# Strassen over all tokens for the output projection, and the second norm inside the MLP

## The chip, the cores and the metric

The kernel runs on one core of a Trainium2 chip. The metric is the device time of one execution in microseconds (us), given as the median of several runs. A profile of one execution is used to see where the time goes. The engines are TensorE (PE; its weight loads are PEld), VectorE (DVE), ScalarE (ACT), GpSimd (POOL) and SyncE (SP), which here issues nearly all transfers.

## The reference, cut to what matters

One decoder layer for 1024 tokens of width 1024: a norm and one large projection, two attention branches, their gated merge, an output projection with a residual, and an MLP of width 4096 with a squared relu. The change lies in the last lines.

```python
merged = g_a * (o_a @ w_up_dil) + g_b * (o_b @ w_up_sb)     # (1024 tokens, 1024)
x  = x + merged @ w_out                                      # output projection
h2 = rmsnorm(x, norm_mlp_g)                                  # x * rsqrt(mean(x*x) + eps) * g
x  = x + jnp.square(jax.nn.relu(h2 @ w_mlp_in)) @ w_mlp_out  # MLP
return rmsnorm(x, norm_final_g)
```

## The kernel before, in words

**Number format.** Everything is held transposed: features on the 128 partitions, tokens along the free axis, in tiles of 128 x 512. A product in float32 accuracy is made of three matmuls. Each operand is split into a high half (a ScalarE copy into the rounded type fp32r) and a low half (a VectorE subtraction, operand minus high half); the three are high x high, high x low and low x high (`mm3`, `product`). So each operand of each product costs one ScalarE and one VectorE operation.

**Strassen.** Large products use the Strassen-Winograd form on 2 x 2 blocks: seven block products in place of eight, with four sums or differences of the left (weight) blocks, `s1` to `s4` (`lefts`), four of the right (activation) blocks, `t1` to `t4`, and additions of the results. A *pair* is two output tiles. The products are taken in the order 0, 1, 5, 6, 4, 3, 2; products 0 and 1 need only plain blocks, and the others need sums or differences.

**Stages after the attention.** (1) The up products of the stick-breaking branch: for each of 8 tiles and each half of the tokens (`c`), 12 matmuls, then a VectorE multiplication with the gate and an addition give `mg[c][j]`. (2) The output projection. For the tokens 0 to 511 it is Strassen with the token halves 0 to 255 and 256 to 511 as the two block columns (`out_pair`); POOL makes its differences `t1` to `t4` (tiles `tw`, `WC[0]` is 'p'), and VectorE the sums of weights. For the tokens 512 to 1023 it is plain, in two quarters of 256 tokens. Each result is added to a tile `x1` of the residual, which also goes to memory (`xdr`). (3) The second norm: for each of the three parts of the tokens, `squares` sums the squares over the features (ScalarE squares, VectorE adds over groups of `GW` tiles, a matmul with ones sums over partitions, tile `ss`), `rstd` takes the root and spreads it over the partitions by a matmul with the identity (tile `rb`), and VectorE multiplies `x1` by the gain and by `rb`. (4) From these normalized tiles come the seven right operands `hm` of the hidden layer (`operands`), for the last 512 tokens in two halves. (5) The hidden layer has 16 pairs of 84 matmuls each (7 products of 4 k and 3 matmuls). The first products (0 and 1) of `NE` = 4 pairs are begun early, before the operands 2 to 6 are ready (`hidden_first`, `hidden_11`). `finish` is relu and square, both on ScalarE; for the block `b12` it is a ScalarE relu and a VectorE multiplication. The results go to memory (`udr`). (6) The down projection, Strassen too, and the final norm.

**The order of the work.** Nothing is issued where the program text stands. Each call is recorded in a plan (`Plan.record`), and `Plan.issue` places the instructions on the engines by a list schedule: TensorE's recorded order gives each matmul a position in time, every other instruction a due time worked back from what needs it, and an engine takes the ready instruction that is due first. Three limits hold it: a window by engine (how far ahead of the oldest unstarted instruction it may reach; `WMLP` holds after the attention), a slack added to the due times, and the tiles: 102 slots of 128 x 512 (`NSLOT`) and 8 banks of PSUM. All instructions are issued through one helper, so every row of the profile has the line L388, and the rows are told apart by the names of tiles: `bank` is an accumulator, `ws` a block of weights with its sums and halves, `gl` the gated products, `msh`/`msl` the halves of `mg`, `hh`/`hl` the halves of the hidden layer's operands, `pk` a hidden block, `x` a tile of the residual, `sq` squares.

Of the kernel before, what the change touches and what calls it, by code (L numbers as in the profile page):

```python
# [9 lines left out]
F32 = mybir.dt.float32  # L10
# [29 lines left out]
MC = 0  # L40
OPE = "pd"
HPE = (0, 0)
DPE = "d"
WC = 'pd'
# [9 lines left out]
GW = 8  # L54
GT = 8
LW = False
# [5 lines left out]
WMLP = {'pe': 45000.0, 'act': 15000.0, 'dve': 40000.0, 'pool': 30000.0, 'sync': 40000.0}  # L62
# [4 lines left out]
NE = 4  # L67
FIRST = 2
STEPS = (1, 3, 4, 5, 6)
EARLY = (5, 6, 7, 7, 7)  # L70
# [321 lines left out]
def hybrid_block(ctx, tc, xT, w_t, w_vn, w_up, w_o, w_mi, w_mo, gains, bgate, out):  # L392
# [861 lines left out]

    plan.window = WMLP
    mg = [[None] * 8 for _ in range(2)]
# [8 lines left out]
    for c, j in [(c, j) for c in range(2) for j in range(8)] if MC else [(c, j) for j in range(8) for c in range(2)]:  # L1265
        if c == 0:
            wu[j] = weight(w_up[j][:, 2:6], 4, "wu", e=WLE[2])
        ps = bank()
        proj(ps, wu[j], oo[c])
        gt = gated(ps, 1, j, c)  # L1270
        dve.tensor_add(gt, gt, ga[c][j])
        mg[c][j] = gt if c == 0 else split(gt, "ms")
# [5 lines left out]
    wo = [None] * 8  # L1278
    x1 = [[None] * 8 for _ in range(2)]
    h2 = [u2("h2n", F32) for _ in range(8)]  # L1280
    hm = [None] * 7

    def finish(t):
        act.activation(t, t, AF.Relu)
        act.activation(t, t, AF.Square)
# [5 lines left out]
    def hidden_11(m, b0, b1):  # L1291
        product(b0, m[0], hm[0], True)
        b11 = keep(b0)
        product(b1, m[1], hm[1], True)
        dve.tensor_add(b11, b11, b1)
        finish(b11)
        return b11

    def pairs():
        return [u2("tc", F32).rearrange("p (k t) -> p k t", k=2) for _ in range(2)]  # L1300

    def one(ts):
        return [t[:, i] for t in ts for i in range(2)]

    def operands(b12, b22, sl, e):

        t1, t2, t3, t4 = (pairs() for _ in range(4))

        def sub(d, x, y):
            for i in range(len(d)):  # L1310
                e.tensor_sub(d[i], x[i], y[i])

        def part(m, t):
            for (hi, lo), x in zip(hm[m], one(t)):
                act.activation(hi[:, sl], x, AF.Copy)
                dve.tensor_sub(lo[:, sl], x, f(hi[:, sl]))

        sub(one(t1), one(b12), [t[:, sl] for t in h2[0:4]])
        sub(t2, b22, t1)
        part(5, t2)  # L1320
        yield
        sub(t3, b22, b12)
        part(6, t3)
        yield
        part(4, t1)
        yield
        sub(one(t4), [t[:, sl] for t in h2[4:8]], one(t2))
        part(3, t4)
        yield
        part(2, b22)  # L1330


    def wide():
        return u2("tw", F32).rearrange("p (k t) -> p k t", k=2)

    def parts(ts):

        return [(x[0][:, i], x[1][:, i]) for x in [halve3(t) for t in ts] for i in range(2)]

    def halve3(t):  # L1340
        hi, lo = (u2("tw").rearrange("p (k t) -> p k t", k=2) for _ in range(2))
        act.activation(hi, t, AF.Copy)
        dve.tensor_sub(lo, t, f(hi))
        return hi, lo

    tw = [[wide() for _ in range(2)] for _ in range(4)]
    top = [(t[:, 0:256], t[:, 256:512]) for t in mg[0]]
    low = [(u2("msh"), u2("msl")) for _ in range(4)]
    for k in range(4):
        (b11, b12), (b21, b22) = top[k], top[k + 4]  # L1350
        t1, t2, t3, t4 = (t[k // 2][:, k % 2] for t in tw)
        for d, x, y in ((t1, b12, b11), (t2, b22, t1), (t3, b22, b12), (t4, b21, t2)):
            eng(WC[0]).tensor_sub(d, x, y)
    first = []
    for k in range(4):
        hi, lo = u2("msh"), u2("msl")
        act.activation(hi[:, 0:256], top[k][0], AF.Copy)
        dve.tensor_sub(lo[:, 0:256], top[k][0], f(hi[:, 0:256]))
        first.append((hi[:, 0:256], lo[:, 0:256]))
    for k in range(4):  # L1360
        act.activation(low[k][0], mg[0][k + 4], AF.Copy)
        dve.tensor_sub(low[k][1], mg[0][k + 4], f(low[k][0]))
    wr = [first] + [[(hi[:, 256 * i:256 * i + 256], lo[:, 256 * i:256 * i + 256]) for hi, lo in low] for i in range(2)]
    p1, p2, p3, p4 = (parts(tw[m]) for m in range(4))
    wr = [wr[0], wr[1], wr[2], p4, p1, p2, p3]

    def out_pair(j):

        for i in range(2):
            x1[0][j + i] = u2("x1", F32)  # L1370
            sync.dma_start(x1[0][j + i], xT[j + i, :, 0:512])
        blocks = load_blocks([w_o[j + i][:, 4 * m:4 * m + 4] for i in range(2) for m in range(2)])
        am = lefts(*blocks, eng=eng(WC[1]))
        for i, pair in ((0, (am[0], am[1])), (1, (halve_w(blocks[2]), am[3]))):
            wo[j + i] = [(hi[:, k], lo[:, k]) for hi, lo in pair for k in range(4)]
        b0, b1, b2 = (bank()[:, 0:256] for _ in range(3))
        for b, m, n, i, h in ((b0, 0, 1, 0, 0), (b1, 1, 1, 0, 0), (b0, 5, 0, 1, 0), (b2, 6, 1, 1, 1), (b0, 4, 0, 1, 1),
                              (b2, 3, 0, 1, 0), (b0, 2, 0, 0, 1)):
            product(b, am[m], wr[m], n > 0)
            xt = x1[0][j + i][:, 256 * h:256 * h + 256]  # L1380
            dve.tensor_add(xt, xt, b)

    for c, o, n in ((0, 0, 512), (1, 0, 256), (1, 256, 256)):
        ssq, add = squares(n // 128, 8, GW, LW and o > 0)
        cs = slice(o, o + n)
        if o:
            early = []
            for m in range(2, 7):
                hm[m] = [(u2("hh"), u2("hl")) for _ in range(4)]
            steps = operands(*later, slice(0, 256), eng(OPE[0]))  # L1390
        for j in range(8):
            if c == 0 and j % 2 == 0:
                out_pair(j)
            if o == 0 and c:
                x1[c][j] = u2("x1", F32)
                sync.dma_start(x1[c][j], xT[j, :, 512 * c:512 * c + 512])
            xt = x1[c][j][:, cs]
            if c:
                ps = bank()[:, 0:n]
                proj(ps, wo[j], [(x[0][:, cs], x[1][:, cs]) for x in mg[c]])  # L1400
                dve.tensor_add(xt, xt, ps)
            if o + n == 512:
                sync.dma_start(xdr[c, j], x1[c][j])
            add(xt)
            if o:
                if j in STEPS:
                    next(steps, None)
                while len(early) < NE and j >= EARLY[len(early)]:
                    early.append(hidden_first(len(early)))
        rs, _ = rstd(ssq, n // 128)  # L1410
        if o:
            early = [(m, b0, hidden_11(m, b0, b1)) for m, b0, b1 in early]

# [206 lines left out]
```

## Time and profile before

| | us |
|---|---|
| median of 3 runs | 1456.57 (1455.22 to 1458.94) |
| the profiled execution | 1458.5 |
| its span, first to last instruction | 1456.7 |
| TensorE matmul busy in the span | 1422.6 (98%) |
| VectorE busy | 1144.7 (79%) |
| ScalarE busy | 784.9 (54%) |
| POOL busy | 202.5 (14%) |

Matmuls are pipelined: a matmul's recorded time overlaps the next one's, so TensorE's rate is read from the distance between starts. A row of the profile names an operation as *out<-in*, gives the shape, the number of such operations, their busy time, the mean length of one in ns, and the idle time of the engine before them with what ended it.

### The profile page before, as it was taken

To read this page: it belongs to the slowest core of one execution; us is meant where nothing else is said; L and a number is where in the kernel's file an instruction comes from. 1 tells how busy PE (TensorE), PEld (TensorE's weight loads), DVE (VectorE), ACT (ScalarE), POOL (GpSimd) and SP (SyncE) were. 2 spreads that over 40 slices of the span, in tenths; PEclk is the share of its full clock that TensorE was granted. 3 is DMA by queue.
4 is the path that set the end of the run, shared out by engine and by line. 5 is a ranking of instruction groups with operands and counts; after the bars stand their busy time and mean duration, and the time that the engine had idled before them with its cause. 6 is when DMAs were issued, how large, how long until landed. Compare 5 with 4: busy or idle time off the path is not lost.

```text
span 1456.7 us, 21968 instructions
## 1 busy us (share of the span) xinstructions
PE 1422.6 (98%) x7432; PEld 1209.7 (83%) x7432; DVE 1144.7 (79%) x1968; ACT 784.9 (54%) x1650; POOL 202.5 (14%) x196
## 2 busy tenths in 40 slices
PE   9999999999999998999999999999999999999997
PEld 9987888888788876888889978888888788888887
DVE  7876887776887868789898898666666969798976
ACT  7656776664655544585453565544555625252632
POOL 2452322322311232010210300000000000000000
PEclk9999999999999999999999999999999999999999
DMA  6247646665245624568032435444446945362703
GB/s 225 65 155 249 209 156 217 218 230 192 64 143 181 200 91 132 178 205 299 32 105 84 162 116 181 148 154 155 148 152 233 345 128 189 104 215 65 253 1 116
DMA packets 133808, 236.60 MB, mean 162 GB/s; under 512 B 16608, under 2 KB 24128, under 8 KB 133696
## 3 DMA queue, kind: packets, MB, share of 16 engines
q1 hardware_dynamic: 131648, 228.91, 46.6%
q0 software_dynamic: 2048, 6.29, 1.4%
q8 instruction: 58, 0.95, 0.3%
q14 instruction: 54, 0.44, 0.1%
HBM read 160.03 MB, written 75.12 MB: 161 GB/s over the span
## 4 chain that ended last, share of the span: by engine, by line
PE 87%; DMA 5%; DVE 4%; ACT 1%; issue 1%; SPq 0%; POOL 0%; DVEq 0%; ACTq 0%; POOLq 0%
PE bank L388 72%; PE vps L388 5%; PE po L388 3%; PE sc L388 3%; PE tr L388 3%; DMA qs<-pdr 1%; DMA pdr<-pl 1%; DVE be L388 1%; DMA pdr<-ph 1%; DVE ws L388 1%; DMA gdr<-gt 0%; SPq L388 0%; PE rb L388 0%; DMA udil<-ut 0%; DVE tw L388 0%
## 5 line engine op out<-in xcount | busy, mean ns | idle before, releaser
L388 PE MATMUL bank<-hh,ws 128*128 128x512 f32 x2016 | 647.2, 394 | 5.1 <-DVE pk L388 4.2
L388 PEld LDWEIGHTS bank<-hh,ws 128*128 128x128 f32 x2016 | 376.4, 188 | 82.1 <-DVE pk L388 5.3
L388 PE MATMUL bank<-hl,ws 128*128 128x512 f32 x1008 | 396.8, 394 | 0.0
L388 DVE TENSOR_TENSOR ws<-ws 128x512 fp32r<-128x512 f32 (+1 forms) x540 | 363.5, 707 | 39.0 <-ACT ws L388 15.5
L388 ACT ACTIVATE ws<-ws 128x512 fp32r<-128x512 f32 x396 | 232.8, 624 | 133.6 <-DVE ws L388 87.7
L388 PE MATMUL bank<-hi,ws 128*128 128x512 f32 (+1 forms) x960 | 281.6, 377 | 2.0 <-DVE x L388 2.0
L388 PEld LDWEIGHTS bank<-hl,ws 128*128 128x128 f32 x1008 | 190.1, 189 | 36.6
L388 PEld LDWEIGHTS bank<-hi,ws 128*128 128x128 f32 x960 | 177.1, 189 | 35.4 <-DVE x L388 2.4
L388 PE MATMUL bank<-lo,ws 128*128 128x512 f32 (+1 forms) x480 | 180.7, 376 | 0.0
L388 POOL TENSOR_TENSOR ws<-ws 128x512 f32<-128x512 f32 x80 | 118.5, 1489 | 329.5 <-DVE ws L388 63.3
L388 DVE TENSOR_TENSOR pk<-pk,bank 128x512 f32<-128x512 f32 x108 | 74.0, 686 | 87.4 <-PE bank L388 63.8
L388 DVE TENSOR_TENSOR x<-x,bank 128x512 f32<-128x512 f32 (+1 forms) x164 | 95.7, 587 | 54.9 <-PE bank L388 54.5
L388 ACT ACTIVATE pk<-bank 128x512 f32<-128x512 f32 x110 | 65.4, 595 | 91.8 <-PE bank L388 79.6
L388 ACT ACTIVATE pk<-pk 128x512 f32<-128x512 f32 x96 | 60.3, 628 | 84.0 <-DVE pk L388 83.5
L388 PEld LDWEIGHTS bank<-lo,ws 128*128 128x128 f32 x480 | 90.7, 189 | 16.5 <-DVE lo L388 0.3
L388 ACT ACTIVATE hi<-ub 128x512 fp32r<-128x512 f32 x112 | 64.7, 622 | 45.5 <-PE bank L388 42.6
L388 ACT ACTIVATE eh<-tr 128x512 fp32r<-128x512 f32 (+3 forms) x140 | 65.8, 498 | 38.3 <-PE tr L388 28.7
L388 DVE TENSOR_TENSOR lo<-ub,hi 128x512 fp32r<-128x512 f32 x112 | 72.2, 686 | 2.3 <-ACT hi L388 2.2
L388 DVE SCALAR_TENSOR_TENSOR el<-tr,eh 128x512 fp32r<-128x512 f32 (+1 forms) x96 | 50.9, 550 | 22.9 <-ACT eh L388 6.4
L388 PE MATMUL sc<-kk,qs 128*128 128x128 f32 (+2 forms) x196 | 61.4, 330 | 4.9 <-DMA qs<-pdr 2.5
L388 PE MATMUL bank<-msh,ws 128*128 128x256 f32 x352 | 65.2, 283 | 0.0
L388 PE MATMUL po<-eh,vs 128*128 128x512 f32 (+2 forms) x196 | 58.5, 309 | 2.8 <-ACT eh L388 1.4
(140 smaller groups left out, 1957.2 us busy)
## 6 DMA issues: line engine op xcount, KB each, us to landing
ub<-udr SPq DMA_DIRECT2D x112, 256.0 KB
ws<-in_w_t_dram SPq DMA_DIRECT2D x80, 256.0 KB
ws<-in_w_mi_dram SPq DMA_DIRECT2D x72, 256.0 KB
udr<-tc SPq DMA_DIRECT2D x64, 256.0 KB
ws<-in_w_mo_dram SPq DMA_DIRECT2D x64, 256.0 KB
udr<-pk SPq DMA_DIRECT2D x48, 256.0 KB
pdr<-ph SPq DMA_DIRECT2D x40, 256.0 KB
pdr<-pl SPq DMA_DIRECT2D x40, 256.0 KB
```

Of the source, the lines that this page charges most:

```text
L388: o[1](*o[2], **o[3])
```

## The change

The output projection becomes one Strassen product over all tokens: its block columns are the token halves 0 to 511 and 512 to 1023, a pair is the output tiles k and k + 4, and two pairs are worked on in turn (`out_group`), product by product. The up products are taken in the order k, k + 4 so that a complete set of four blocks is there after each k, and its four differences and seven splits are written there, the differences on VectorE (`TE`). The second norm is no longer applied ahead of the hidden layer: ScalarE multiplies `x1` by the gain alone (`hs`), the operands are made of that (`operands(k)`), and the root is applied to the positive part, `finish`: max with 0 and multiplication by `rsb` in one VectorE operation, then ScalarE's square. `GW` goes from 8 to 4, `NE` from 4 to 3, ScalarE's window from 15 to 30 us, and the slack after the attention from 14 to 30 us.

```diff
-GW = 8
+GW = 4
-WMLP = {'pe': 45000.0, 'act': 15000.0, 'dve': 40000.0, 'pool': 30000.0, 'sync': 40000.0}
+WMLP = {'pe': 45000.0, 'act': 30000.0, 'dve': 40000.0, 'pool': 30000.0, 'sync': 40000.0}
+MSLACK = 30000.0
-NE = 4
+NE = 3
+TE = 'd'
+HTE = 'd'
...
     plan.window = WMLP
+    plan.slack = MSLACK
...
+    wr = [[] for _ in range(7)]
+    for k in range(4):
+        for j in (k, k + 4):
             wu[j] = weight(w_up[j][:, 2:6], 4, "wu", e=WLE[2])
+            for c in range(2):
+                ps = bank()
+                proj(ps, wu[j], oo[c])
+                gt = gated(ps, 1, j, c)
+                dve.tensor_add(gt, gt, ga[c][j])
+                mg[c][j] = gt
+        b11, b21, b12, b22 = mg[0][k], mg[0][k + 4], mg[1][k], mg[1][k + 4]
+        t1, t2, t3, t4 = (u2("tw", F32) for _ in range(4))
+        wr[0].append(split(b11, "ms"))
+        wr[1].append(split(b21, "ms"))
+        for d, x, y in ((t1, b12, b11), (t2, b22, t1), (t3, b22, b12), (t4, b21, t2)):
+            eng(TE).tensor_sub(d, x, y)
+        for m, t in ((5, t2), (6, t3), (4, t1), (3, t4), (2, b22)):
+            wr[m].append(split(t, "ms"))
...
-    def finish(t):
-        act.activation(t, t, AF.Relu)
+    def finish(t, c, src=None):
+        dve.scalar_tensor_tensor(t, t if src is None else src, 0.0, rsb[c], op0=ALU.max, op1=ALU.mult)
         act.activation(t, t, AF.Square)
...
+    def out_group(ks):
+        x, a, s, ps = {}, {}, {}, {}
+        for k in ks:
+            a[k] = load_blocks([w_o[k + 4 * i][:, 4 * m:4 * m + 4] for i in range(2) for m in range(2)])
+            x[k] = [[u2("x1", F32) for _ in range(2)] for _ in range(2)]
+            for i in range(2):
+                for c in range(2):
+                    sync.dma_start(x[k][i][c], xT[k + 4 * i, :, 512 * c:512 * c + 512])
+        for m in (0, 1, 5, 6, 4, 3, 2):
+            for k in ks:
+                a11, a12, a21, a22 = a[k]
+                if m == 0:
+                    ps[k] = [bank(), mm_tile("bank"), bank()]
+                if m == 5:
+                    s[k] = s1, s2, s3, s4 = [block(4) for _ in range(4)]
+                    dve.tensor_add(s1, a21, a22)
+                    dve.tensor_sub(s2, s1, a11)
+                    dve.tensor_sub(s3, a11, a21)
+                    dve.tensor_sub(s4, a12, s2)
+                left = {0: a11, 1: a12, 3: a22}.get(m) or s[k][{5: 1, 6: 2, 4: 0, 2: 3}[m]]
+                b = ps[k][{1: 1, 6: 2, 3: 2}.get(m, 0)]
+                product(b, halve_w(left), wr[m], m in (0, 1, 6))
+                (x11, x12), (x21, x22) = x[k]
+                for d in {0: (x11,), 1: (x11,), 5: (x21,), 6: (x22,), 4: (x22,), 3: (x21,), 2: (x12,)}[m]:
+                    dve.tensor_add(d, d, b)
+                for i, c in {1: ((0, 0),), 4: ((1, 1),), 3: ((1, 0),), 2: ((0, 1),)}.get(m, ()):
+                    t = x[k][i][c]
+                    sync.dma_start(xdr[c, k + 4 * i], t)
+                    sums[c][1](t)
+                    hs[k][i][c] = u2("hs", F32)
+                    act.activation(hs[k][i][c], t, AF.Copy, scale=gsb[:, 1, k + 4 * i:k + 4 * i + 1])
+            yield
+
+    def operands(k):
+        (b11, b12), (b21, b22) = hs.pop(k)
+        t1, t2, t3, t4 = (u2("tc", F32) for _ in range(4))
+        hm[0].append(split(b11, "h"))
+        hm[1].append(split(b21, "h"))
         for d, x, y in ((t1, b12, b11), (t2, b22, t1), (t3, b22, b12), (t4, b21, t2)):
-            eng(WC[0]).tensor_sub(d, x, y)
...
+            eng(HTE).tensor_sub(d, x, y)
+        for m, t in ((5, t2), (6, t3), (4, t1), (3, t4), (2, b22)):
+            hm[m].append(split(t, "h"))
+
+    hs = {k: [[None] * 2 for _ in range(2)] for k in range(4)}
+    sums = [squares(4, 8, GW) for _ in range(2)]
+    for _ in out_group((0, 1)):
+        pass
+    operands(0)
+    for i, _ in enumerate(out_group((2, 3))):
+        if i == 2:
+            operands(1)
+    early = [hidden_first(p) for p in range(NE)]
+    operands(2)
+    operands(3)
+    for c in range(2):
+        act.activation(rsb[c], rstd(sums[c][0], 4)[0], AF.Copy)
+    early = [(m, b0, hidden_11(m, b0, b1)) for m, b0, b1 in early]
...
         product(b0, am[2], hm[2], False)
         b12 = u2("relu", F32)
-        act.activation(b12, b0, AF.Relu)
-        dve.tensor_mul(b12, b12, b0)
+        finish(b12, 1, b0)
```

In `hidden_pair` the other blocks call `finish` with the half of the tokens that they belong to: `b11` and `b21` with 0, `b22` and `b12` with 1.

## Rows read from the trace of the kernel before

**Rows 1.** The page, parts 1 and 2: busy time by engine; granted clock by slice.
```profile
PE 1422.6 (98%) x7432; PEld 1209.7 (83%) x7432; DVE 1144.7 (79%) x1968; ACT 784.9 (54%) x1650; POOL 202.5 (14%) x196
...
PEclk9999999999999999999999999999999999999999
```

**Rows 2.** Windows: length; busy (count) of PE, PEld, DVE, ACT, POOL; clock; DMA.
```profile
689.00:711.00 22.00, 22.00 (x99) 18.21 (x98) 17.00 (x27) 6.59 (x12) 3.15 (x4) 1.00 0.22 72
711.00:733.00 22.00, 22.00 (x99) 18.22 (x98) 21.16 (x36) 13.67 (x27) 8.12 (x8) 1.00 0.12 36
733.00:745.00 12.00, 9.91 (x70) 8.58 (x69) 11.90 (x18) 3.63 (x8) 5.43 (x6) 1.00 0.19 68
745.00:856.00 111.00, 111.00 (x815) 105.90 (x814) 96.89 (x210) 58.77 (x125) 11.97 (x12) 1.00 0.33 110
856.00:870.00 14.00, 12.59 (x56) 10.11 (x55) 13.26 (x26) 8.78 (x16) 0.00 (x0) 1.00 0.43 144
870.00:1147.00 277.00, 277.00 (x1224) 229.18 (x1223) 192.73 (x302) 150.96 (x270) 0.00 (x0) 1.00 0.54 184
1147.00:1157.00 10.00, 8.00 (x28) 5.86 (x27) 10.00 (x18) 1.84 (x4) 0.00 (x0) 0.83 1.05 403
```

**Rows 3.** The chain of waits, 690 to 900 us: start, length, what.
```profile
689.85 37.87 PE bank L388 x167
...
732.98 2.29 DVE msl L388 x2
...
743.93 41.30 PE bank L388 x341
...
857.63 0.70 DVE pk L388
```

**Rows 4.** TensorE's timeline at the three holes: idle time and releaser in brackets.
```profile
741.79 1.91 PE L388 MATMUL bank<-tw,ws 128*128 128x256 f32 x13 [1.22 <-DVE x L388]
...
858.37 0.50 PE L388 MATMUL bank<-hh,ws 128*128 128x512 f32 x1 [1.41 <-DVE pk L388]
...
1152.72 0.50 PE L388 MATMUL bank<-hi,ws 128*128 128x512 f32 x1 [2.00 <-DVE x L388]
```

**Rows 5.** Groups by shape, TensorE, 733 to 835 us: the output projection.
```profile
L388 PE MATMUL bank<-msh,ws 128*128 128x256 f32 x352 | 65.2, 283 | 0.0
L388 PE MATMUL bank<-msl,ws 128*128 128x256 f32 x176 | 49.5, 284 | 0.0
L388 PE MATMUL bank<-tw,ws 128*128 128x256 f32 x192 | 26.8, 287 | 2.1 <-DVE x L388 1.2 <-DVE tw L388 0.5 <-DVE ws L388 0.2
```

**Rows 6.** TensorE's timeline: a dense run of 256 columns, and one sum of squares.
```profile
754.11 3.04 PE L388 MATMUL bank<-tw,ws 128*128 128x256 f32 x24
...
785.07 0.95 PE L388 MATMUL ss<-ones,sq 128*128 128x1 f32 x8
```

**Rows 7.** VectorE's timeline: an idle spell, an operation beside POOL, dense runs.
```profile
692.38 0.69 DVE L388 TENSOR_TENSOR gl<-gl,bank 128x512 f32<-128x512 f32 x1 [1.43 <-PE bank L388]
...
711.11 1.23 DVE L388 TENSOR_TENSOR ws<-ws 128x512 f32<-128x512 f32 x1
...
767.01 2.49 DVE L388 TENSOR_TENSOR ws<-ws 128x512 f32<-128x512 f32 x4
...
863.86 3.09 DVE L388 TENSOR_TENSOR ws<-ws 128x512 fp32r<-128x512 f32 x5
```

**Rows 8.** Groups by shape, VectorE, 783 to 835 us: the root's small operations.
```profile
L388 DVE SCALAR_TENSOR_TENSOR sm<-sm 128x4 f32<-128x4 f32 x2 | 0.3, 160 | 0.0
```

**Rows 9.** Groups by shape, 870 to 1147 us: the hidden pairs' additions, relu and squares.
```profile
L388 DVE TENSOR_TENSOR pk<-pk,bank 128x512 f32<-128x512 f32 x42 | 28.9, 687 | 53.3 <-PE bank L388 47.2 <-ACT pk L388 6.1
L388 DVE TENSOR_TENSOR relu<-relu,bank 128x512 f32<-128x512 f32 x15 | 10.3, 687 | 18.5 <-ACT relu L388 18.5
...
L388 ACT ACTIVATE pk<-pk 128x512 f32<-128x512 f32 x84 | 52.7, 628 | 80.4 <-DVE pk L388 79.9
```

More of the change, by code (lines that the diff above doesn't have):

```diff
@@ L39 @@
 PL = "d"
-MC = 0
-OPE = "pd"
 HPE = (0, 0)
 DPE = "d"
-WC = 'pd'
 JE = "d"
@@ L53 @@
 G0 = 4
-GW = 8
 GT = 8
-LW = False
+GW = 4
 LT = True
@@ L66 @@
 CSLACK = 40000.0
-NE = 4
+MSLACK = 30000.0
+NE = 3
+TE = 'd'
+HTE = 'd'
 FIRST = 2
-STEPS = (1, 3, 4, 5, 6)
-EARLY = (5, 6, 7, 7, 7)
 CHUNKS = (4, 4, 4, 4)
@@ L1264, in hybrid_block @@
     wu = [None] * 8
-    for c, j in [(c, j) for c in range(2) for j in range(8)] if MC else [(c, j) for j in range(8) for c in range(2)]:
-        if c == 0:
+    wr = [[] for _ in range(7)]
+    for k in range(4):
+        for j in (k, k + 4):
             wu[j] = weight(w_up[j][:, 2:6], 4, "wu", e=WLE[2])
[L1268 to L1272, printed above, removed]
+            for c in range(2):
[12 more added lines that the diff above has]
+            wr[m].append(split(t, "ms"))
     xdr = dram.tile([2, 8, 128, 512], F32, name="xdr")
     udr = dram.tile([16, 7, 128, 512], F32, name="udr")
[L1278 to L1281, printed above, removed]
-    def finish(t):
-        act.activation(t, t, AF.Relu)
+    hm = [[] for _ in range(7)]
+    rsb = [u2("rsb", F32) for _ in range(2)]
+    def finish(t, c, src=None):
+        dve.scalar_tensor_tensor(t, t if src is None else src, 0.0, rsb[c], op0=ALU.max, op1=ALU.mult)
         act.activation(t, t, AF.Square)
@@ L1295, in hidden_11 @@
         dve.tensor_add(b11, b11, b1)
-        finish(b11)
         return b11
[L1299 to L1330, printed above, removed]
@@ L1333, in wide @@
[L1333 to L1347, printed above, removed]
@@ L1348, in hybrid_block @@
[L1348 to L1351, printed above, removed]
-        for d, x, y in ((t1, b12, b11), (t2, b22, t1), (t3, b22, b12), (t4, b21, t2)):
-            eng(WC[0]).tensor_sub(d, x, y)
[L1354 to L1412, printed above, removed]
-        def norm(ts, ks):
-            for k in ks:
-                dve.scalar_tensor_tensor(ts[k], x1[c][k][:, cs], gsb[:, 1, k:k + 1], rs, op0=ALU.mult, op1=ALU.mult)
-        if c == 0:
-            norm(h2, range(8))
-            for m in range(2):
-                hm[m] = [split(t, "h") for t in h2[4 * m:4 * m + 4]]
-            continue
-        b12, b22 = (pairs() for _ in range(2))
-        if o == 0:
-            norm(one(b12) + one(b22), range(8))
-            later = b12, b22
-            continue
-        for _ in steps:
-            pass
-        norm(one(b12) + one(b22), range(8))
-        for _ in operands(b12, b22, cs, eng(OPE[1])):
-            pass
@@ L1444, in hidden_pair @@
             am = lefts(*blocks, m, eng("p" if HPE[0] <= p < HPE[1] else "d"))
+        finish(b11, 0)
         b2 = bank()
@@ L1451, in hidden_pair @@
         dve.tensor_add(b22, b22, b2)
-        finish(b22)
+        finish(b22, 1)
         product(b2, am[3], hm[3], False)
         dve.tensor_add(b21, b21, b2)
-        finish(b21)
+        finish(b21, 0)
         product(b0, am[2], hm[2], False)
         b12 = u2("relu", F32)
-        act.activation(b12, b0, AF.Relu)
-        dve.tensor_mul(b12, b12, b0)
+        finish(b12, 1, b0)
         if last:
```

## The prediction

> **What bounds the kernel now.** I read the page first [rows 1]: TensorE is busy 98% of the span at full granted clock, VectorE 79%. The windows around the change come next [rows 2]; the reader is to see that TensorE has next to no idle time there, save two holes, while VectorE is at 17.00 of 22, 21.16 of 22, 11.90 of 12, 96.89 of 111 and 13.26 of 14 us, together 160.2 of 181 us (88.5%), and only later, in the hidden pairs, at 192.73 of 277 (70%). The chain of waits [rows 3] says the same in order of time: it runs on TensorE's own matmuls, and leaves them only from 727.7 to 743.9 us, for VectorE (the operand tiles `tw`, `msl`, `ws`), and at 857 us. The timeline [rows 4] shows these holes on TensorE. So the stretch is TensorE-bound with VectorE close behind, and each microsecond of matmul taken out brings VectorE nearer to being the bound.
>
> What the holes cost: matmuls of 256 columns start 0.120 us apart ((3.04 - 0.28)/23, [rows 6]), those of 512 columns 0.2263 us apart (277.00/1224, [rows 2]). From 733 to 745 us 70 of 256 were issued: 12.00 - 70 x 0.120 = 3.6 us lost. From 856 to 870 us 56 of 512: 14.00 - 56 x 0.2263 = 1.3 us lost. A third hole, at 1150 us where the down projection begins, is 10.00 - 28 x 0.2263 = 3.7 us with its spell of lower clock [rows 2, 4].
>
> **TensorE's part of the change.** Before, the output projection is Strassen on 512 tokens in quarters of 256 columns (4 pairs x 7 products x 4 k x 3 = 336 matmuls) and plain on the rest (8 tiles x 2 halves x 8 k x 3 = 384). The trace has exactly these, 352 + 176 + 192 = 720 of 256 columns [rows 5]. 720 x 0.120 = 86.4 us. After: 4 pairs x 7 x 4 x 3 = 336 of 512 columns, 336 x 0.2263 = 76.0 us. Removed: 10.4 us. The column sums of the squares go from one group of 8 to two groups of 4 for each half of the tokens: 4 float32 matmuls (8 records) take 0.95 - 0.06 = 0.89 us [rows 6]. Before 0.89 + 0.45 + 0.45 = 1.8 us, after 4 x 0.89 = 3.6: added 1.8 us. The broadcasts of the root (`rb`) stay 8 matmuls, 1.8 us. The hidden products are the same 1344 matmuls: that three pairs instead of four are begun early moves 24 matmuls (5.4 us) behind the rest and removes none. TensorE's net: -10.4 + 1.8 = -8.6 us, all on the path, because TensorE is the path.
>
> What the trace says of the width is the sum above: two matmuls of 256 columns cost 0.240 us, one of 512 costs 0.226. The Trainium skill (TensorE: Matmul & The Clock Gate, section "Wait — 56ns, not 53.3ns?") has a warm matmul start N/2.4 GHz + 2.5 ns after the last one, which estimates 109 and 216 ns; then width gives almost nothing, the projection would go from 78.6 to 72.5 us, and TensorE's net would be -4.3 us instead of -8.6 (a total of about 1451.7). The rows disagree at both widths by 11 ns, so I go by them.
>
> **VectorE's part, step by step.** Dense VectorE operations on 512 columns start 0.60 us apart ((2.49 - 0.69)/3 and (3.09 - 0.69)/4, [rows 7]), though each lasts 0.69. I count, after the change, from 689.4 us (the up products that make `mg`: 192 matmuls, 43.4 us before 733) up to the fifth-operand product of hidden pair 0, the first that needs a sum or difference of the normalized tiles:
> - up products: 32 for gate and sum, 6 remaining low halves of `wu`, 16 Strassen differences (until now POOL's, in halves of 256), 28 low halves of right operands: 82.
> - output projection: per pair 4 sums and 7 low halves of weights, 7 additions into `x1`, 3 of squares: 84 in all. A low half of `w_o` that only the plain part needed is gone.
> - operands of the hidden layer, per k 4 differences and 7 low halves: 44. The eight 512-wide and sixteen 256-wide normalizations are gone from VectorE; ScalarE scales by the gain instead (16 operations), and is at 59 of 111 us [rows 2].
> - early pairs: 6 low halves of weights and 3 additions; pair 0's own weights: 3 before that product; 12 in all. The 3 finishes are not counted, since no product waits for them; the two chains of the root, of five small operations at 0.16 us each [rows 8], are 1.6 us.
> SP's transfers are the same in number (16 tiles each of `x`, `w_o` and `xdr`), in groups of two pairs instead of one; the DMA engines are at a third of their time there [rows 2], so I cost them at nothing; a late block would show as a wait of ScalarE for `ws`.
> Together 222 x 0.602 + 1.6 = 135.2 us. TensorE in the same stretch: 43.4 + 76.0 + 3.6 + 1.8 + 72 x 0.2263 = 141.1 us. So VectorE would be needed at 96% if TensorE never stood still. The rows show it at 95% and more only where TensorE stood still (733 to 745, 856 to 870 us) or just before. I take 93%, between the 88.5% of the whole stretch and those 95 to 99%: 135.2/0.93 = 145.4, that is 4.3 us of new holes. The ends: 0, and at 88.5% 152.8 - 141.1 = 11.7 us.
>
> The old holes (3.6 and 1.3 us) are inside this stretch and their causes go: the first product now needs only the four splits of `b11`, which are ready k by k during the up products, and the differences are first needed two products (2 x 24 x 0.2263 = 10.9 us) into the projection; with two pairs in turn, an addition out of a bank has 12 matmuls of another bank (2.7 us) as cover against 0.7 us. That VectorE has idle spells of 1.4 us early in the up products, with "PE bank" as releaser [rows 7], is where the difference work can go; ScalarE's window of 30 instead of 15 us lets the high halves come that early. POOL's differences leave, and with them VectorE operations of 1.23 us beside them [rows 7]. What is late next is the tail: after the last product the sum into `x12`, ScalarE's scaling, two differences, a split (some 3 x 0.6 + 2 x 0.69 + latencies, about 5 us) stand before pair 0's fifth product, under 16.3 us of early products. This cover also holds the root (two chains of ScalarE, VectorE and 1.8 us of `rb`), which no longer stands before any product: only `finish` waits for it.
>
> **Hidden pairs.** `finish` moves its relu to VectorE, with the factor: 4 VectorE operations a pair for 1 until now, so 22 instead of 19; ScalarE loses 3 [rows 9]. 3 x 0.602 x 14.6 pairs in 870 to 1147 us is 26 us on an engine with 84 us idle there: 79% afterwards, hidden under 19.0 us of matmuls a pair. No row shows a max-and-multiply out of PSUM; by the nearest, the addition out of a bank (0.687 us long) it costs as any other, so between 0.60 and 0.75 us; at 0.75 it is 31 us, hidden still. If that cover were gone all of it would stand on the path. The hole at 1150 us I leave as it is (between -3.7 and +2).
>
> **The sum.** -8.6 - 4.9 + 4.3 = -9.2 us. The profiled execution took 1458.5 us (span 1456.7 and 1.8 around it); that is 1.9 above the median of the runs, 1456.57. So 1449.3 for the profiled execution, and 1447.4 for the median. Bounds of the likeliest case: 1456.6 - 13.5 = 1443.1 without new holes, and with 8.6 us of them (VectorE at 90%) 1451.7.
>
> **Rivals.**
> - VectorE becomes the bound (88.5% is all it reaches): -8.6 - 4.9 + 11.7 = -1.8, 1454.8. For it: the mean of rows 2. Against: that mean has the stretch from 745 to 856 us, where it idled because nothing was asked of it.
> - Each VectorE operation costs its whole length, 0.69 us: 222 x 0.69 + 1.6 = 154.8, 13.7 us of holes, 1456.8. Against it stand four operations in 2.49 us [rows 7]. The Trainium skill (VectorE: DVE Perf Modes, section "The DRAIN you can't avoid") has such a rule, that the next operation waits until the pipe is empty; the trace does not agree at 0.60 us apart.
> - Slower: the tile slots. The code has 102. The right operands of the projection live until its last group and hold 56, those of the hidden layer hold another 56, and weights and `x1` need their own: they cannot all live at once. If the operand work of k = 0 and 1 (22 operations) cannot be placed before the projection ends, VectorE owes then 44 + 12 operations and the root, 35.3 us, and 9 more for pair 0's weights and additions, 40.7 us, against 16.3 us of early products and 10.9 us of pair 0's first four: 13.5 us of waiting, and as long again (some 5 us) while pairs 1 and 2, also shorter by 5.4 us, give it no time to catch up. -13.5 + 13.5 + 5 = +5, 1461.6. It decides from about 33 of the 44 operations being late. Against: products of the second group free 8 slots at each of the seven steps.
> - Nothing is late, and the hole at 1150 us shrinks by 2 as well: 1441.
>
> **The numbers.** Likeliest 0.62 (1443 to 1452), nothing late 0.12, VectorE-bound 0.14, whole lengths 0.04, slots 0.08. 0.3% of the median is 4.4 us, about what a measurement of this kernel can tell from no change: faster means under 1452.2, slower above 1460.9. Faster: 0.60 + 0.12 + 0.03 = 0.75; same: 0.02 + 0.11 + 0.04 = 0.17; slower 0.08. The range 1441 to 1455 leaves out the slots, the whole lengths, and a little at either end: 0.18.
>
> **What would show it.** Right: no 256-column matmuls in the projection, 336 of 512 columns in some 76 us; VectorE over 93% from 689 us to the first pairs; holes of a few microseconds with VectorE as releaser; no hole at the start of the projection; hidden pairs at 19.0 us each. Wrong: a hole above 5 us in one place, above all between the last output product and pair 0; VectorE idle while TensorE waits (then it is slots or order, not VectorE's load); hidden pairs longer than 19 us.

## The result, and the profile after

The changed kernel takes 1440.86 us (median of 4, 1436.99 to 1443.22) against 1457.16 us for the kernel before on the same chip (median of 4, 1455.22 to 1458.94): ratio 0.9884, interval 0.9868 to 0.9901. The forecast was 1447.4 us, faster; the sign is right, the gain of 16.3 us is nearly twice the 9.2 us forecast, and the time lies 0.1 us below the range.

The profiled execution after took 1436.99 us (span 1435.2), against 1458.5 (1456.7) before. That is 21.5 us apart, more than the medians, so the first thing to settle is where the two spans part. TensorE's timeline of the kernel before, at an up product of wave 1 and at the projection's first product (start, length, what):
```profile
654.31 0.47 PE L388 MATMUL bank<-ooh,wu 128*128 128x512 f32 x1
...
732.98 0.28 PE L388 MATMUL bank<-msh,ws 128*128 128x256 f32 x1
```
The same two places after, and the two holes that are left up to the down projection (idle time and releaser in brackets):
```profile
648.55 0.48 PE L385 MATMUL bank<-ooh,wu 128*128 128x512 f32 x1
...
727.25 0.39 PE L385 MATMUL bank<-msh,ws 128*128 128x512 f32 x1
...
747.78 0.73 PE L385 MATMUL bank<-msh,ws 128*128 128x512 f32 x2 [0.43 <-DVE ws L385]
...
835.06 0.50 PE L385 MATMUL bank<-hh,ws 128*128 128x512 f32 x1 [0.69 <-ACT pk L385]
```
Up to the first of these places both programs issue the same instructions in the same order on every engine, and yet they are 5.8 us apart there. That is a difference between executions, as e1 and e4 show below, and no effect of the change. From the projection's first product to the end of the span it is 1456.7 - 733.0 = 723.7 us before and 1435.2 - 727.2 = 708.0 us after: 15.7 us, near the 16.3 of the medians. All that follows is measured on this stretch, called the **tail** below.

The page of the changed kernel, parts 1 and 2 (compare [rows 1]):
```profile
PE 1409.8 (98%) x7064; PEld 1186.2 (83%) x7064; DVE 1162.5 (81%) x1962; ACT 774.1 (54%) x1591; POOL 173.3 (12%) x168
...
PEclk9999999999999999999999999999999999999998
```
Windows of the changed kernel, columns as in [rows 2] (length; busy (count) of PE, PEld, DVE, ACT, POOL; clock; DMA). They are the up products, the start of the projection, its rest, the early hidden products, the first hidden pairs, the other pairs, and the beginning of the down projection:
```profile
705.00:727.20 22.20, 22.20 (x99) 18.39 (x98) 20.84 (x34) 7.03 (x12) 0.00 (x0) 1.00 0.00 0
727.20:748.00 20.80, 20.37 (x90) 16.56 (x90) 20.35 (x35) 12.61 (x22) 0.00 (x0) 1.00 0.39 135
748.00:807.00 59.00, 59.00 (x273) 49.09 (x273) 55.13 (x90) 40.75 (x71) 0.00 (x0) 1.00 0.34 118
807.00:834.00 27.00, 27.00 (x133) 22.76 (x131) 25.74 (x51) 12.29 (x23) 0.00 (x0) 1.00 0.40 127
834.00:848.00 14.00, 13.31 (x59) 10.73 (x58) 12.84 (x22) 7.51 (x13) 0.00 (x0) 1.00 0.30 95
848.00:1117.00 269.00, 269.00 (x1189) 222.73 (x1188) 211.47 (x337) 123.32 (x219) 0.00 (x0) 1.00 0.52 180
1117.00:1135.00 18.00, 18.00 (x81) 14.92 (x80) 16.87 (x28) 10.89 (x20) 0.00 (x0) 1.00 0.80 286
```
The reader is to see three things. VectorE is at 134.9 of the 143.0 us from 705 to 848 (94%), and TensorE stands still for a microsecond in them. The hidden pairs have no holes: 269.00/1189 = 0.2262 us a matmul, VectorE at 211.47 of 269 (79%). And the last window, where the down projection begins, is full: the hole of [rows 2, 4] at 1150 us is gone, and with it its spell of lower clock.

Groups by shape of TensorE from 727 to 812 us after, in place of [rows 5]: 224 + 112 = 336 matmuls of 512 columns, none of 256.
```profile
L385 PE MATMUL bank<-msh,ws 128*128 128x512 f32 x224 | 69.8, 391 | 0.4 <-DVE ws L385 0.4
L385 PE MATMUL bank<-msl,ws 128*128 128x512 f32 x112 | 43.6, 390 | 0.0
```
Groups by shape of VectorE from 848 to 1117 us after, in place of [rows 9]: the maximum with the factor, in place and out of a bank, beside an addition out of a bank.
```profile
L385 DVE SCALAR_TENSOR_TENSOR pk<-pk,rsb 128x512 f32<-128x512 f32 x44 | 30.3, 688 | 0.7
L385 DVE TENSOR_TENSOR pk<-pk,bank 128x512 f32<-128x512 f32 x43 | 29.5, 687 | 44.1 <-PE bank L385 37.1 <-ACT pk L385 6.8
L385 DVE SCALAR_TENSOR_TENSOR relu<-bank,rsb 128x512 f32<-128x512 f32 x14 | 9.6, 688 | 1.5 <-PE bank L385 1.5
```
The chain of waits after, 805 to 900 us (compare [rows 3]): the sums (`ss`) and the broadcasts of the root (`rb`) stand between products, TensorE does not wait for the root, and the chain leaves TensorE once, for 0.61 us.
```profile
805.41 5.38 PE bank L385 x23
810.79 0.79 PE ss L385 x8
811.58 1.00 PE rb L385 x8
812.58 2.73 PE bank L385 x12
815.31 0.89 PE rb L385 x8
816.20 18.18 PE bank L385 x80
834.41 0.61 ACT pk L385
835.06 65.12 PE bank L385 x286
```

### The profile page after: what moved, and what is told of

Read it like the earlier page. It is cut to its first block, busy times and chain, and to the rows that moved or that the text cites. A ratio compares the mean times of both kernels' runs of the same rounds, so it can differ in the third digit from the quotient of the medians.

```text
span 1435.2 us, 21197 instructions
## 1 busy us (share of the span) xinstructions
PE 1409.8 (98%) x7064; PEld 1186.2 (83%) x7064; DVE 1162.5 (81%) x1962; ACT 774.1 (54%) x1591; POOL 173.3 (12%) x168
## 4 chain that ended last, share of the span: by engine, by line
PE 88%; DVE 5%; DMA 4%; ACT 1%; issue 1%; SPq 0%; POOL 0%; DVEq 0%; ACTq 0%; POOLq 0%
PE bank L385 73%; PE vps L385 5%; PE po L385 3%; PE sc L385 3%; PE tr L385 3%; DVE be L385 1%; DMA gdr<-gt 1%; DVE ws L385 1%; DMA pdr<-pl 1%; DMA qs<-pdr 1%; PE rb L385 1%; PE ss L385 0%; DVE el L385 0%; DMA pdr<-ph 0%; DMA udil<-ut 0%
## 5 line engine op out<-in xcount | busy, mean ns | idle before, releaser
L385 PEld LDWEIGHTS bank<-hh,ws 128*128 128x128 f32 x2016 | 376.4, 188 | 79.6 <-ACT pk L385 2.4
L385 DVE TENSOR_TENSOR ws<-ws 128x512 fp32r<-128x512 f32 (+1 forms) x536 | 356.8, 699 | 60.6 <-PE bank L385 30.1
L385 PEld LDWEIGHTS bank<-lo,ws 128*128 128x128 f32 x480 | 90.3, 188 | 16.3
L385 ACT ACTIVATE pk<-pk 128x512 f32<-128x512 f32 x48 | 30.3, 630 | 95.1 <-DVE pk L385 95.1
L385 ACT ACTIVATE hi<-ub 128x512 fp32r<-128x512 f32 x112 | 67.7, 629 | 17.6 <-DMA ub<-udr 11.9
L385 PE MATMUL bank<-msh,ws 128*128 128x512 f32 x224 | 69.8, 391 | 0.4 <-DVE ws L385 0.4
```

The costliest lines, as they stand in the source:

```text
L385: o[1](*o[2], **o[3])
```

## The experiments

Two explanations stood after the comparison. One: the gain is that of the new arithmetic (wider products, the norm behind the hidden layer), and I had sized it too small. The other: a good part comes from the two numbers of the planner that the change also sets (ScalarE's window in `WMLP` 15 to 30 us, the slack 14 to 30 us), which the prediction priced at nothing of their own. The tail of every profile is given as "first product to end"; where a run has one execution, it is this figure that is compared, not the total.

**e1_again: the changed kernel once more**, no edit, as a control.

> The changed kernel once more, as a control. Theory: of the 21.5 us between the two profiled executions, 5.8 us lie before 660 us, where the two kernels issue the same instructions, and are a difference between executions; 15.7 us lie in the changed part. So the ratio to the kernel before should be 0.987 to 0.990 (14 to 19 us less). Rival: the early 5.8 us belong to the change; then the first 600 us of this profile end some 6 us earlier than those of the kernel before again, and the ratio is near 0.985.

Measured: 1439.86 us, ratio 0.9875, interval 0.9857 to 0.9892. TensorE's timeline at the projection's first product:
```profile
730.17 0.39 PE L385 MATMUL bank<-msh,ws 128*128 128x512 f32 x1
```
It comes 2.9 us later than in the first profile of the same program, and the span of 1438.2 us ends 708.0 us behind it, as the first did. So the tail repeats within 0.1 us, while the stretch ahead of it wanders by some us. e4 below, which has the changed kernel's first part too, reached the up product of 648.55 us only at 655.84, later than the kernel before: the early 5.8 us are not the change's.

**e2_before_settings: the kernel before with both new planner numbers.**
```diff
-WMLP = {... 'act': 15000.0, ...}
+WMLP = {... 'act': 30000.0, ...}
...
     plan.window = WMLP
+    plan.slack = 30000.0
```

> The kernel before with only two numbers of the change: ScalarE's window after the attention 30 us for 15, and the slack after the attention 30 us for 14. Theory S: the hole of 3.7 us where the down projection begins (1150 us) was one of order, and these two numbers close it: the hole falls under 0.5 us, 1453 to 1454 us, ratio 0.997 to 0.998. Rival C: the hole went because finish and the norm moved between engines; then it stays at 2 to 4 us here and the ratio is 1.000 (0.999 to 1.001).

Measured: 1451.24 us, ratio 0.9952 (0.9938 to 0.9965); tail 717.2 us, 6.5 less than before. The planner's numbers by themselves are worth that much without any of the new arithmetic.

**e7_before_act30: the kernel before with ScalarE's window alone** (the first half of the diff above).

> The kernel before with ScalarE's window alone at 30 us. From the projection's first product to the end it took 723.7 us before and 717.2 with both numbers. Theory W: 717 to 718 us, the holes at 736 to 745 and at 1150 us gone. Rival L: 723 to 724 us.

Measured: 1450.95 us in one execution (the kernel before, same chip, 1458.43); tail 717.3 us. So it is ScalarE's window, and the slack adds nothing here. How it works is seen on ScalarE's timeline, at the first high half of a `w_o` block. The kernel before:
```profile
719.58 0.62 ACT L388 ACTIVATE ws<-ws 128x512 fp32r<-128x512 f32 x1
```
and with the wider window:
```profile
701.98 0.62 ACT L388 ACTIVATE ws<-ws 128x512 fp32r<-128x512 f32 x1
```
Counted back from the projection's first product (732.98 and 731.90 us) it comes 29.9 us ahead for 13.4, 16.5 us earlier, and VectorE can make the low halves in spells that it idled through before. Windows of this kernel, columns as in [rows 2]:
```profile
688.00:710.00 22.00, 22.00 (x99) 18.23 (x98) 19.09 (x32) 9.26 (x19) 3.06 (x4) 1.00 0.29 85
732.00:744.00 12.00, 12.00 (x102) 12.00 (x101) 10.05 (x18) 4.29 (x7) 6.39 (x6) 1.00 0.06 21
1146.00:1156.00 10.00, 10.00 (x46) 8.29 (x45) 9.25 (x16) 4.92 (x9) 0.00 (x0) 1.00 1.06 395
```
Against [rows 2]: VectorE 19.09 of 22 us where it had 17.00, TensorE 12.00 of 12 where it had 9.91, and 10.00 of 10 at the down projection where it had 8.00. Two of the three old holes close, one is new (at 824.7 us, 1.07 us, for `sq` on VectorE), and the one of the first hidden pairs stays at 1.5 us.

At the down projection the operands are hidden blocks, split again: high halves `hi` on ScalarE, low halves `lo` on VectorE. Shown are the last high halves of this stage on ScalarE's timeline and, on VectorE's, the seven low halves ahead of the addition into `x` for which TensorE stands still at 1150.7 us [rows 4]. The kernel before:
```profile
1141.17 3.74 ACT L388 ACTIVATE hi<-ub 128x512 fp32r<-128x512 f32 x7
...
1147.16 4.30 DVE L388 TENSOR_TENSOR lo<-ub,hi 128x512 fp32r<-128x512 f32 x7
```
and with the wider window:
```profile
1133.22 5.83 ACT L388 ACTIVATE hi<-ub 128x512 fp32r<-128x512 f32 x11
...
1141.59 4.30 DVE L388 TENSOR_TENSOR lo<-ub,hi 128x512 fp32r<-128x512 f32 x7
```
Counted from the projection's first product, the high halves end at 407.2 us for 411.9 and the low halves at 414.0 for 418.5, while TensorE begins the down projection only 2.4 us earlier (392.6 for 395.0). So VectorE has gained 2.1 us on TensorE there, and the 2.00 us of idle time are gone. That it is the earlier high halves which move VectorE's work is read from this order and not tested by itself.

**e3_after_oldset, e5_after_act15, e6_after_slack14: the changed kernel with old planner numbers**, both, the window alone, the slack alone.
```diff
-WMLP = {... 'act': 30000.0, ...}      (e3, e5)
+WMLP = {... 'act': 15000.0, ...}
-MSLACK = 30000.0                      (e3, e6)
+MSLACK = 14000.0
```

> The changed kernel with the two numbers of the kernel before (ScalarE's window 15 us, slack 14 us). Theory S: the hole where the down projection begins is back, 3 to 4 us, and with ScalarE's high halves later some 1 to 4 us of holes in the up products and the projection: 4 to 8 us slower than the changed kernel, ratio to the kernel before 0.991 to 0.994. Rival C: no hole there, as fast as the changed kernel, 0.988.

> The changed kernel with ScalarE's window back at 15 us, the slack left at 30. Measured from the projection's first product to the last instruction, where executions of one kernel agree (708.0 us twice for the changed kernel, 719.3 with both numbers of before). Theory W, the window does it, since the holes with both numbers of before end on ScalarE's high halves: 716 to 720 us, holes in the projection and at the down projection. Rival L, the slack does it: 708 to 710 us.

> The changed kernel with the slack back at 14 us, ScalarE's window left at 30. From the projection's first product to the end: theory W 708 to 710 us; rival L 716 to 720 us; if each closes one of the two holes, 711 to 716 us, and the place of the hole says which.

Measured: e3 1451.28 us, ratio 0.9953 (0.9936 to 0.997), tail 719.3; e5 tail 734.9 (one execution, 1468.56 us); e6 tail 712.2 (one execution, 1443.28 us). The changed kernel needs the new numbers: without them it gains 4.4 us of tail instead of 15.7, and with the old window beside the new slack it is 11 us slower than the kernel before. So the two parts do not add up: the numbers alone are worth 6.5 us and the arithmetic alone 4.4, both together 15.7. The slack, worth nothing to the kernel before, is worth 712.2 - 708.0 = 4.2 us here. TensorE's timeline of e3, holes for ScalarE in the projection and one at the down projection:
```profile
743.11 0.50 PE L385 MATMUL bank<-msh,ws 128*128 128x512 f32 x1 [1.29 <-ACT ws L385]
...
752.70 0.47 PE L385 MATMUL bank<-msh,ws 128*128 128x512 f32 x1 [1.74 <-ACT hs L385]
...
1145.49 0.50 PE L385 MATMUL bank<-hi,ws 128*128 128x512 f32 x1 [2.02 <-DVE x L385]
```
In e5 one hole is 7.7 us. ScalarE's timeline there:
```profile
742.86 1.83 ACT L385 ACTIVATE msh<-tw 128x512 fp32r<-128x512 f32 x3 [3.04 <-DVE tw L385]
744.60 2.17 ACT L385 ACTIVATE ws<-ws 128x512 fp32r<-128x512 f32 x4
```
and TensorE's:
```profile
745.27 0.79 PE L385 MATMUL bank<-msh,ws 128*128 128x512 f32 x1 [7.73 <-ACT ws L385]
```
The high halves that TensorE needs (`ws`, 744.60) come behind copies of differences (`msh<-tw`), which wait 3.04 us for VectorE, although the blocks of `w_o` that they are made of were called from memory by 679 us. In this trace ScalarE takes its instructions in the planned order, and what waits at the head holds up what stands behind it; that a tile slot for the copy was free earlier is not shown. A part of e5's loss is the clock: from 731.9 to 765 us TensorE was granted 0.79 of it on the mean, at most 33.1 x 0.21 = 7.0 us. Why the new slack makes this worse than the old one is left open.

**e4_cols256: the changed kernel, its projection in products of 256 columns**: the same three matmuls of each term, once for each half of the bank.
```diff
-                product(b, halve_w(left), wr[m], m in (0, 1, 6))
+                product_halves(b, halve_w(left), wr[m], m in (0, 1, 6))
...
+        for o in (0, 256):
+            cs = slice(o, o + 256)
...
+                pe.matmul(bank[:, cs], hi, bm[i][0][:, cs], ...)
```

> The changed kernel with each product of the output projection issued as two products of 256 columns, 672 matmuls for 336. By the rows (0.120 us for 256 columns, 0.2263 for 512) the projection grows by 672 x 0.120 - 336 x 0.2263 = 4.6 us, ratio about 0.9915. Rival: a matmul costs its columns and 2.5 ns; then it grows by 0.9 us, ratio about 0.989. A third way: the longer projection gives VectorE cover, and small holes shrink by up to 0.6 us.

Measured: 1445.73 us, ratio 0.9912 (0.9897 to 0.9928); tail 711.0. The projection in a window, first e4, then the changed kernel:
```profile
734.60:818.50 83.90, 83.69 (x697) 83.31 (x696) 79.67 (x132) 53.80 (x94) 0.00 (x0) 1.00 0.38 127
```
```profile
727.20:806.80 79.60, 79.17 (x361) 65.50 (x361) 75.48 (x124) 53.16 (x93) 0.00 (x0) 1.00 0.35 123
```
The width is worth 83.9 - 79.6 = 4.3 us in the projection, 672 matmuls of 256 against 336 of 512; by the distances between starts of [rows 2, 6] it is 672 x 0.120 - 336 x 0.2263 = 4.6. Half the width also means twice as many weight loads: they are busy 83.31 of 83.90 us in e4 and 65.50 of 79.60 in the changed kernel, and e4 does not tell the one from the other. The end moves by 3.1 us and not by 4.3, because the hole at 835 us, which ended with ScalarE's `pk`, is gone in e4 (1.0 us of it); the holes in the projection cost about the same in both.

**e8_norm_ahead: the changed kernel with the norm ahead of the hidden layer**: the tiles wait for both roots, VectorE scales them by gain and root, and `finish` is as before.
```diff
-                    hs[k][i][c] = u2("hs", F32)
-                    act.activation(hs[k][i][c], t, AF.Copy, scale=gsb[...])
+                    hs[k][i][c] = t
...
+    rbs = [rstd(sums[c][0], 4)[0] for c in range(2)]
...
+                dve.scalar_tensor_tensor(t, hs[k][i][c], gsb[...], rbs[c], op0=ALU.mult, op1=ALU.mult)
...
+        operands(k)
```

> The changed kernel with the norm put back ahead of the hidden layer, for all tokens at once: VectorE multiplies the 16 tiles of the residual by gain and root, the operands are made of these, finish is again ScalarE's relu and square. Theory N, the norm inside the MLP is what allows one projection over all tokens: no hidden product can start before the root, so TensorE waits for an addition, a square, the sums, the root with its table load, the broadcast, a multiplication and a split, some 9 us, and then for VectorE, which owes 16 multiplications and 44 operand operations (some 36 us) against 27 us of early products: 15 to 25 us slower than the changed kernel; 723 to 733 us from the projection's first product to the end, where the changed kernel takes 708.0. Rival: the early products and the later finish were cover enough, and the norm costs 5 us or less: 708 to 713.

Measured: 1454.64 us, ratio 0.9991 (0.9971 to 1.0011); tail 720.8, that is 12.9 us more. The loss is a little smaller than expected and lies where it was put. The operands of the first two k, which the changed kernel makes during the projection, stand behind the root here as well. TensorE's timeline:
```profile
813.47 1.19 PE L385 MATMUL ss<-ones,sq 128*128 128x1 f32 x8 [2.19 <-DVE sq L385]
...
818.15 2.07 PE L385 MATMUL rb<-ident,sm 128*128 128x128 f32 x8 [1.57 <-DVE sm L385]
...
838.70 0.50 PE L385 MATMUL bank<-hl,ws 128*128 128x512 f32 x1 [1.15 <-DVE hl L385]
```
Windows, columns as in [rows 2]:
```profile
811.00:838.00 27.00, 22.79 (x100) 18.69 (x98) 24.53 (x49) 17.39 (x32) 0.00 (x0) 0.87 0.06 21
838.00:856.00 18.00, 14.18 (x52) 8.92 (x53) 18.00 (x31) 9.78 (x17) 0.00 (x0) 1.00 0.04 15
```
The root stands in front of the products again (idle for `sq`, then for `sm`, and the granted clock of this window is 0.87), and then VectorE, which has 16 scalings more, is busy 18.00 of 18 us while TensorE waits for `hl`. With one projection over all tokens there is no second half whose products could stand beside the root: the new projection without the norm's new place is worth next to nothing (2.9 us of tail), and it is 3.6 us slower than the kernel before with the same planner numbers (e2, 717.2). Of the 12.9 us, at most 27.0 x 0.13 = 3.5 are the lower clock. The other half, the norm's new place with the old projection, was not run; nor were `GW`, `NE` and the move of the differences from POOL to VectorE varied one by one.

**e9_single: one pair of tiles at a time** in the projection, in place of two in turn.
```diff
-    for _ in out_group((0, 1)):
-        pass
+    for k in (0, 1):
+        for _ in out_group((k,)):
+            pass
...
-    for i, _ in enumerate(out_group((2, 3))):
+    for i, _ in enumerate(out_group((2,))):
...
+    for _ in out_group((3,)):
+        pass
```

> The changed kernel with one pair of tiles at a time in the projection instead of two in turn. Theory: two pairs double the time before the differences and the banks are needed again (5.4 us for 2.7); without it the same operations are late: holes of 3 to 8 us in the projection, 711 to 716 us from its first product to the end. Rival: 2.7 us cover 0.7 us of addition anyway, 708 to 709.

Measured: tail 727.2 us (one execution, 1462.27): 19.2 more than the changed kernel, where 3 to 8 were expected. It is not a sum of short waits for banks. Windows:
```profile
783.00:793.00 10.00, 1.56 (x7) 1.02 (x6) 9.05 (x14) 2.81 (x6) 0.00 (x0) 0.79 0.03 12
793.00:833.40 40.40, 33.88 (x133) 26.42 (x133) 23.26 (x37) 20.01 (x34) 0.00 (x0) 0.93 0.41 142
```
VectorE's timeline:
```profile
788.24 2.94 DVE L385 TENSOR_TENSOR hl<-tc,hh 128x512 fp32r<-128x512 f32 x4
```
and TensorE's:
```profile
792.68 1.22 PE L385 MATMUL bank<-msh,ws 128*128 128x512 f32 x2 [8.44 <-DVE ws L385]
```
VectorE makes `hl`, which no product reads before 819.7 us, while TensorE waits 8.4 us for `ws`; afterwards VectorE itself is busy 23.26 of 40.40 us. That is order (or slots), not load. Which of the two puts the work in that order was not tested. The lower clock of the two windows is at most 10.0 x 0.21 + 40.4 x 0.07 = 4.9 of the 19.2 us.

**e10_vec16, e11_vec32: more VectorE work in the changed kernel.** e10 computes the 16 differences of the projection's operands twice, e11 those of the hidden operands as well: 16 x 0.602 = 9.6 and 19.3 us of VectorE added.
```diff
+            eng(TE).tensor_sub(d, x, y)      (e10, e11: the line doubled)
...
+            eng(HTE).tensor_sub(d, x, y)     (e11: the line doubled)
```

> The changed kernel with each of the 16 differences of the projection's right operands computed twice by VectorE: 16 x 0.602 = 9.6 us more of VectorE work in the up products and the projection. Theory of the forecast, VectorE can be used to 93%: 144.8/0.93 - 141.1 = 14.6 us of holes there, 13 us more than now: 720 to 722 us. Rival: VectorE can be used to the full as long as what is late can be put off, so that only what exceeds TensorE's time counts: 144.8 - 141.1 = 3.7 us, 709 to 712 us.

> The same with the 16 differences of the hidden layer's operands doubled too, 19.3 us more of VectorE work in all. Theory of the forecast: 154.5/0.93 - 141.1 = 25.0 us of holes, 730 to 733 us. Rival, only what exceeds TensorE's time: 154.5 - 141.1 = 13.4 us, 719 to 722 us.

Measured: tails 716.7 and 721.4 us (one execution each, 1449.47 and 1455.97): +8.7 and +13.4. Neither theory holds for both: the ceiling of 93% is too dear both times, "only the excess over TensorE" is too cheap for e10 and fits e11. Windows of e10:
```profile
731.00:751.00 20.00, 17.27 (x66) 12.65 (x65) 19.77 (x34) 7.72 (x14) 0.00 (x0) 0.91 0.06 23
751.00:762.00 11.00, 8.46 (x34) 5.68 (x33) 11.00 (x19) 5.22 (x9) 0.00 (x0) 1.00 0.92 287
762.00:819.00 57.00, 57.00 (x265) 47.52 (x264) 54.31 (x90) 40.85 (x71) 0.00 (x0) 1.00 0.30 108
```
The first 9.6 us fall where VectorE is full already (20.35 of 20.80 us in the changed kernel) and the end comes 8.7 us later. The second 9.7 fall on the later stretch, which has spells free, and cost 4.7. These are not prices of VectorE's load alone: in e10 at most 20.0 x 0.09 = 1.8 us are the lower clock, and the added operations move other work too (the DMA engines, at 0.39 of their time in the changed kernel's first 20.8 us of the projection, are here at 0.06 and then at 0.92). What the runs do show is that no one ceiling for the whole stretch describes VectorE: in the changed kernel it is full for 20 us, and TensorE stands still for 0.43. That what counts is how much it owes where TensorE next needs something from it is the reading that fits, not a thing tested.

**e12_wide45_gw8: a try for more**: ScalarE's window 45 us, and the sums of squares in groups of 8.
```diff
-WMLP = {... 'act': 30000.0, ...}
+WMLP = {... 'act': 45000.0, ...}
-GW = 4
+GW = 8
```

> A version that might beat both: the changed kernel with ScalarE's window at 45 us for 30 and the squares summed in one group of 8 again (GW = 8). The sums then take 2 x 0.89 us for 4 x 0.89: 1.8 us less. Theory: only that is left, since the changed kernel's holes from the projection to the down projection are 2 us in all: 705 to 707 us from the projection's first product to the end (708.0 now), ratio to the kernel before 0.986 to 0.988. Rival: a wider window lets ScalarE take tile slots with work that is far off, and holes grow: 709 us or more.

Measured: 1442.18 us, ratio 0.99 (0.9882 to 0.9919); tail 709.7. It does not beat the changed kernel (tail 708.0, ratio 0.9875 and 0.9884). Its groups of 8 spare TensorE 1.6 us of sums, but 3.4 us more are lost in holes, one of them on TensorE's timeline:
```profile
780.39 0.50 PE L385 MATMUL bank<-msh,ws 128*128 128x512 f32 x1 [1.44 <-ACT ws L385]
```
Going from 30 back to 15 us costs 27 us in e5; going on to 45, with the groups of 8, gains nothing. Which of e12's two edits opens the holes was not tested, so a best place of the window is not shown.

## Why the prediction was right in sign and too small

**TensorE's part: right.** From the first product of the projection to the first hidden product it is 92.9 us before and 79.75 after. What the distances between starts exceed the dense ones by (0.120 and 0.227 us), the cost of the holes with the restart behind each, is 4.2 us of it before and 1.0 after; the sums and broadcasts inside are 2.35 and 2.4. So the matmuls went from 86.3 to 76.3 us, -10.0 against -10.4 forecast. Sums and broadcasts of the second norm together went from 3.1 to 4.9 us, and this term is -8.2 against -8.6. (Counted by starts, one sum is 0.81 us and not the 0.89 of the prediction.) e4 confirms the term's price of width directly, 4.3 us, weight loads included. The Trainium skill's start-to-start rule (TensorE: Matmul & The Clock Gate, section "Wait — 56ns, not 53.3ns?") gives 672 x 109.2 - 336 x 215.8 ns = 0.9 us for the same comparison, an estimate with which the runs do not agree.

**Old holes at the projection and the first pairs: right that they shrink, wrong on why the first does.** The prediction put it down to the operands' new places. e7 shows that the first closes in the kernel before too, with ScalarE's window alone; e3 shows that in the changed kernel 6.5 us are lost in the projection with the old numbers, in spite of the new places. The sentence that the window "lets the high halves come that early" named the mechanism but gave it no price. The second hole is the change's own: it stays at 1.4 to 1.5 us of idle time in the kernel before with the new numbers (e2, e7), and is gone in the changed kernel with the old ones (e3: no idle spell above 0.2 us from 806 to 900 us). In the changed kernel itself 0.69 us of it are left, the hole at 835 us.

**"The hole at 1150 us I leave as it is": the step that failed most.** It had -3.7 as an end of its own bounds, but the sum took 0 and the range's lower end -2; -3.7 is what came. It closes in e7 without any of the new arithmetic, stays closed in e6 with the window alone, and in the changed kernel with the old numbers 5.5 us are lost at that place (e3, 1135 to 1155 us; 2.8 of them idle, the rest restart and lower clock). I had taken it as outside the change, though the window that the diff widens rules the planning of that stage too.

**New holes: mis-sized.** 4.3 us were forecast, from a ceiling of 93% for VectorE. Measured were 1.0 in the projection and 1.1 at the first hidden pairs, 2.1 in all. The load was right: in the stretch that the prediction counted, from the last 192 up products to pair 0's fifth-operand product (683.6 to 826.0 us), VectorE is busy 133.0 of 142.4 us, 93%, where 135.2 of 145.4 were forecast. That a load of 93% makes 4.3 us of holes was not. e10 and e11 show why no such share could carry the sum.

Summed on the tail: matmuls and sums -8.2; the two old holes and the new ones, measured 4.2 + 1.95 before and 2.1 after, -4.0 (forecast -4.9 + 4.3 = -0.6); the seam at 1150 us -3.7 (forecast 0). That is -15.9, and -15.7 was measured. The tail gained 6.5 us more than forecast: 3.7 are the seam and 3.4 the holes, less 0.4 of TensorE's part. Seen the other way, along the runs: the planner's numbers on the kernel before -6.5 (e2), the rest of the change on top of them 717.2 - 708.0 = 9.2. That the second number equals the forecast is chance, since the forecast had the old holes in it and no price for the planner.

**Hidden pairs: right.** 0.2262 us a matmul, VectorE at 79% as worked out, no hole; the maximum with the factor lasts 688 ns, as the addition that it was priced by.

**The rivals.** VectorE as the bound (1454.8) and whole-length operations (1456.8) did not come: VectorE reached 94% where the first let it reach 88.5. The slots' rival did not come either, but its sign, VectorE idle or at work for later while TensorE waits, is what e9 shows: two pairs in turn keep it away, and 2.7 us of cover for a bank was too small a reason for them. "Nothing late and the hole at 1150 us shrinks" (1441) was nearest the result, at a chance of 0.12, and by luck: 2.1 us of holes came where it had none, and the hole gave 3.7 us where it had 2.

## What to carry to other kernels

Where a change also alters how far ahead the instructions are planned, price that by itself: the same two numbers, put on the old kernel alone, were here worth 6.5 of 15.7 us, and without them the new arithmetic kept 4.4. Look at every hole of every stage that such a setting covers, not only at those beside the edit. And compare from a marker in the changed stretch to the end, when the stretch ahead of it wanders more than the effect.

## What the runs showed of the hardware

The stretch ahead of the projection took 727.2 and 730.2 us in two executions of one program, and the kernel before reached the same up product 5.8 us later (654.31 against 648.55) with the same instructions in the same order; the tail behind the marker repeated at 708.0 us. What varies in the first part was not examined.

A maximum with a factor out of a bank lasts 688 ns on 512 columns, the same operation in place 688, and a plain addition out of a bank 687: neither the second operation nor the source in the bank cost anything that shows.
